# Eight in-place shifts moved behind the last chunk of the lead's second half, and one block's weights fetched later

## The chip, the cores and the metric

The kernel runs on one core of one Trainium2 chip. A core has five engines that run their own instruction lists side by side and wait for one another by semaphores: TensorE (PE, matrix products into the PSUM banks), VectorE (DVE, elementwise work on two operands), ScalarE (ACT, one-operand functions and casts), GpSimd (POOL) and SyncE (SP, which here issues most loads). Loads and stores are DMAs, issued by SP, ACT or POOL. The metric is the device time in microseconds of one execution; a change is read against the median of several.

## The reference

One layer of a streaming encoder, on x of 1024 positions by 1024 channels, in float32. Cut to what matters here:

```python
h = rms_norm(x, norm_mix_g) * (1.0 + sc1) + sh1
proj = h @ w_in                                  # 1024 -> 7168 columns
b_s, c_s, v_s, v_c, gl_c, gate_br = split(proj)
y_a = (b_s * dwconv3(c_s * v_s)) @ w_short_out
y_b = silu(layer_norm(dwconv31(v_c * sigmoid(gl_c)))) @ w_conf_out
g_a, g_b = split(sigmoid(gate_br))
x = x + g1 * ((g_a * y_a + g_b * y_b) @ w_o)
...                                              # SwiGLU ffn, final norm
```

The change sits in the preparation of `h` and the first columns of `h @ w_in`.

## The kernel before, in words

**Layout.** Everything is held transposed: channels on the 128 partitions, positions along the row. The 1024 channels are eight chunks of 128 (KC = 8), the 1024 positions two halves of 512 (`halves`, index h). An operand of a product is kept as a high and a low part (`hi` is a rounding cast on ACT, `lo` the rest, a subtraction on DVE), and `mm3` (lines 386 to 397) makes each product from three matmuls: high by high (L394), low activation by high weight (L395), high activation by low weight (L397). Most of the projection afterwards goes by a scheme of seven products for eight (`PRODUCTS`), which needs sums and differences of chunks k and k + 4 in both halves: `b11`, `b12`, `b21`, `b22`.

**The lead.** Before that scheme can start, the kernel computes some columns directly while x is still being prepared: three column blocks of the gate g_b ("lead", tile names `lead`, gate blocks 0 to 2), and, in the first half, four more. This is the loop `for h in range(2)` at line 845 over `row_blocks` (line 515): per chunk k it asks `act_x` (line 660) for the chunk's activation and `lead_w` or `again_w` (line 709) for its weights, and lists the matmuls of all blocks. In the second half (h = 1) the chunks come in the order `SECOND` = 5, 6, 7, 0, 1, 2, 3, 4: the weights of 5, 6, 7 are still there from the first half (`kept`), those of 0 to 4 are fetched again, 128 x 384 each.

**act_x and modulate.** For a chunk of the second half `modulate` (line 474) lists a DVE multiplication by scale and norm (L476, `x<-x,naff,rx1r`), the high part on ACT (L484, `h41h` for chunk 4, half 1), the low part on DVE (L485, `h41l`), and puts a last step aside in the list `shifts`: the shift of x in place on ACT (L491), which the matmuls of the lead do not need but the sums of the later scheme do. `act_x` decides when the shifts are listed: none after the first four chunks, two after each of the next three, and the remaining two after the last, in the order in which they were put aside.

**Weights.** `next_w(ahead)` (line 355) hands out the next prepared weights after `fetch` (line 360) has brought the list `ready` up to ahead + 1 entries of `plan`. Each entry loads a block from DRAM on SP's queue into a raw buffer (five of them), casts the high part on ACT (L231, `wh<-raw`) and subtracts the low part on DVE (L232, `wl<-raw,wh`); there are three high and three low buffers. The plan in this place is: the five lead blocks of chunks 0 to 4, then one full-width block (`w_plain`, the fourth gate block, 128 x 1024), then the weights of the seven-product scheme. `again_w` asks with ahead = 1 for the first chunks and AHEAD = 2 for the last two.

**What follows the lead.** Line 845 on: after the second half, three activations of the first half that were used unsplit are split (`h00` to `h20`, L426 and L427), the three gate blocks go through a sigmoid on ACT (`sig<-lead`, L578) and out to DRAM. Then the loop at `for k in range(KH)` builds the sums of the scheme (L865, L439, L870) and splits `t2` (L434, L435). Then `col_block(next_w(), hT, (0, 1), "gb")` does the plain gate block: 8 chunks, 2 halves, 3 matmuls, 48 in all, tile name `gb`. Then the scheme starts (tile name `bank`).

**Order of the work.** The kernel is written as one long text; a compiler pass lists each engine's instructions from it. By default what is ready, in the pass's own reckoning, goes in the order of the text; `tc.issue_after(ins)` puts what its block lists on the engine of `ins` behind `ins`, and waits for nothing else. Tiles come from pools with a fixed number of buffers: the large pool `tp` has 58 tiles of 128 x 512, from which h, t2 and their parts are taken. At run time each engine goes through its list in order.

Of the kernel before, what the change touches and what calls it, by code (L numbers as in the profile page):

```python
# [44 lines left out]
KC = D // P  # L45
# [31 lines left out]
KEPT = 3  # L77
SECOND = [*range(KC - KEPT, KC), *range(KC - KEPT)]
# [10 lines left out]
AHEAD = 2  # L89
# [40 lines left out]
def block_kernel(ctx: ExitStack, tc: tile.TileContext, x0, xT, c, vecs, ada, w_first, w_plain, w_duals,  # L130
# [38 lines left out]
    def s_tile(name, dt=F32):  # L169
        return hl_tile(name, dt)  # L170
# [30 lines left out]
    def modc(i):  # L201
        return mod[:, i : i + 1]
# [152 lines left out]
    def next_w(ahead=AHEAD):  # L355

        fetch(ahead + 1)
        return ready.pop(0)

    def fetch(n):  # L360
        while plan and len(ready) < n:
            unit = plan.pop(0)
            ready.append(unit() if callable(unit) else weights(*unit))

    def modulation(i, raw=None):

        if raw is None:
            raw = load(ada[i])
        else:
            nc.sync.dma_start(raw, ada[i])  # L370
        modulation_of(i, raw)
# [8 lines left out]
    def affine(dst, k, sc, gains, g):  # L380
        nc.vector.scalar_tensor_tensor(
            out=dst[:, k : k + 1], in0=modc(sc + k), scalar=1.0, in1=gains[:, g + k : g + k + 1],
            op0=ALU.add, op1=ALU.mult,
        )
# [76 lines left out]
    def rstd_negative(ss, r, q, t=None):  # L461

        t = q if t is None else t
        nc.vector.scalar_tensor_tensor(out=t, in0=ss, scalar=EPS, in1=q, op0=ALU.add, op1=ALU.mult)
        nc.vector.scalar_tensor_tensor(out=r, in0=t, scalar=1.5, in1=r, op0=ALU.subtract, op1=ALU.mult)
        return r
# [7 lines left out]
    def modulate(src, r, scale, shift, name, begun=None, later=None):  # L474

        begin = nc.vector.scalar_tensor_tensor(  # L476
            out=src, in0=src if begun is None else begun, scalar=scale, in1=r, op0=ALU.mult, op1=ALU.mult
        )
        if name is None:
            act = nc.scalar.activation(src, src, AF.Identity, bias=shift)  # L480
            modulate.ins = begin.ins, act.ins, begin.ins
            return None
        hi, lo = hl_tile(name + "h"), hl_tile(name + "l")
        act = nc.scalar.activation(hi, src, AF.Identity, bias=shift)  # L484
        last = nc.vector.scalar_tensor_tensor(  # L485
            out=lo, in0=src, scalar=shift, in1=f32(hi), op0=ALU.add, op1=ALU.subtract
        )
        if later is None:
            nc.scalar.activation(src, src, AF.Identity, bias=shift)
        else:  # L490
            later.append(lambda: nc.scalar.activation(src, src, AF.Identity, bias=shift))  # L491
        modulate.ins = begin.ins, act.ins, last.ins
        return hi, lo
# [48 lines left out]
    def squares_x(src, acc=None, clock=(), tile_of=g_tile):  # L542

        for i, t in enumerate(src):
            sq = tile_of("sq")
            act = nc.scalar.activation(sq, t, AF.Square, scale=1.0 / 32.0)
            if acc is None:
                acc = sq
            else:
                add = nc.vector.tensor_tensor(acc, acc, sq, ALU.add)  # L550
                if i in clock:
                    keep_clock(keep_clock.ins, 1, sq)
                    keep_clock(keep_clock.ins, 1, wide=True)
        squares_x.ins = act.ins, add.ins
        return acc
# [87 lines left out]
    def first_x():  # L643

        nonlocal rx_0
        ss, r, q = rx_0
        y, t = x[0, 0], s_tile("newton")
        begin = nc.vector.scalar_tensor_tensor(out=y, in0=xin[0], scalar=naff1[:, :1], in1=r, op0=ALU.mult, op1=ALU.mult)
        nc.vector.scalar_tensor_tensor(out=t, in0=ss, scalar=EPS, in1=q, op0=ALU.add, op1=ALU.mult)
        keep_clock(keep_clock.ins, 1, t)  # L650
        keep_clock(keep_clock.ins, CLOCK[4], wide=True)
        nc.vector.scalar_tensor_tensor(out=y, in0=t, scalar=1.5, in1=y, op0=ALU.subtract, op1=ALU.mult)
        act = nc.vector.tensor_scalar(y, y, modc(0), None, ALU.add)
        with tc.issue_after(act.ins):
            begin = nc.vector.scalar_tensor_tensor(out=r, in0=t, scalar=1.5, in1=r, op0=ALU.subtract, op1=ALU.mult)
        rx_0 = r
        modulate.ins = begin.ins, act.ins, begin.ins
        return y

    def act_x(k, h=0):  # L660
        nonlocal rx_0, rx_1
        if h == 0:
            with ExitStack() as after:
                after.enter_context(tc.issue_after(squares_x.ins[1] if k in (0, X1_AT + 2) else modulate.ins[0]))
                if k == X1_AT + 2:
                    x1_load.append(act_x.last)
                    after.enter_context(tc.issue_after(x1_load[0]))
                for i in range(2 * k, 2 * k + 2):
                    modulation(i, ucp.tile([P, T + CK - 1], F32, tag="uc", name="ada")[:, :D])
            affine(naff1, k, 8, ng, V_GMIX)  # L670
            x[k, 0] = s_tile(f"x{k}0")
            if k == 0:
                return first_x()
        whole = h == 0 and k < WHOLE
        with tc.issue_after(los[-2]) if len(los) > 1 else ExitStack():
            hT[k][h] = modulate(x[k, h], rx_1 if h else rx_0, naff1[:, k : k + 1], modc(k),
                                None if whole else f"h{k}{h}", None if h else xin[k], shifts if h else None)
        if h:
            los.append(modulate.ins[2])
            for _ in range(len(shifts) if len(los) == KC else 2 * (len(los) > KEPT + 1)):  # L680
                with tc.issue_after(modulate.ins[1]):
                    shifts.pop(0)()
        if h == 0:
            if k == X1_AT:
                for i in range(KC):
                    x[i, 1] = s_tile(f"x{i}1")
                    act_x.last = nc.sync.dma_start(x[i, 1], xT[i, :, halves[1]]).ins
            elif k == X1_AT + 1:
                with tc.issue_after(modulate.ins[2]), tc.issue_after(modulate.ins[1]):
                    rx_1 = squares_x([x[i, 1] for i in range(KC)])  # L690
            elif k == X1_AT + 2:
                with tc.issue_after(modulate.ins[2]):
                    rx_1 = rstd_negative(*rx_1)
            if whole:
                return x[k, 0]
        return hT[k][h]

    los, shifts = [], []
# [10 lines left out]
    def again_w(i):  # L709

        if i < KEPT:
            return kept.pop(0)
        return next_w(1 if i < KC - 2 else AHEAD)

    rx_1 = None
    KH = KC // 2
# [128 lines left out]
    for h in range(2):  # L845
        lead = row_blocks(act_x if h == 0 else lambda i: act_x(SECOND[i], 1), GATES if h else LEAD, "lead", ops,
                          again_w if h else lead_w, 1 + h, None if h else half_way, GATES)
        if h == 0:
            ops = [(again_w(i), xs) for i, xs in ((i, act_x(SECOND[i], 1)) for i in range(3))]
        if h:  # L850
            for k in range(WHOLE):
                with tc.issue_after(modulate.ins[2]):
                    hT[k][0] = split(x[k, 0], hl_tile, f"h{k}0")
        for j, ps in enumerate(lead):
            if j < GATES:
                gate("b", j, h, ps)
            else:
                begun[(j - GATES) // 2]((j - GATES) % 2, "2", ps)
# [746 lines left out]
```

## Time and profile before

| | before |
|---|---|
| median of 3 runs | 1467.25 us (1467.06 to 1467.79) |
| profiled execution | 1467.45 us |
| its span, first to last instruction | 1465.7 us |
| PE busy | 1452.0 us, 99% |
| DVE busy | 1183.8 us, 81% |
| ACT busy | 623.7 us, 43% |
| POOL busy | 503.2 us, 34% |

A line of a timeline reads: start in us from the span's start, duration, engine, line of the kernel, operation, output <- inputs, shapes, count; in brackets the idle time before it and what ended that. Rows with xN are several of a kind merged. Durations of neighbours overlap at their ends, so an instruction's cost in a full engine is the distance to the next start. The views used: the page (busy times), the waits of an engine, and timelines of single engines.

### The profile page before, as it was taken

How to read it: one execution, taken by the hardware profiler on the slowest of the kernel's cores; microseconds unless marked ns; L12 is line 12 of the kernel's file. 1: busy time of each engine (PE TensorE's matmuls, PEld its weight loads, DVE VectorE, ACT ScalarE, POOL GpSimd, SP SyncE). 2: the span in 40 equal slices, each digit the busy share in tenths (PEclk: the TensorE clock that was granted, in tenths of full speed). 3: DMA queues.
4: the chain of work that ended last, by engine and by line, in shares of the span. 5: the costliest groups of instructions: out<-in, count | busy, mean ns of one | idle time of the engine just before them, and what ended most of it. 6: DMA issues, size and time to landing. Idle time of an engine off the chain costs nothing.

```text
span 1465.7 us, 17764 instructions
## 1 busy us (share of the span) xinstructions
PE 1452.0 (99%) x6418; PEld 1192.1 (81%) x6418; DVE 1183.8 (81%) x1643; ACT 623.7 (43%) x911; POOL 503.2 (34%) x459
## 2 busy tenths in 40 slices
PE   9999999999999999999999999999999999999997
PEld 4778888888888888888888888888888888888887
DVE  7897999987988979999688798777777665676755
ACT  4773333333333346455225475444444343222335
POOL 0007777677677761111012002111111015435005
PEclk9999999999999999999999999999999999999999
DMA  9542232323222357486595337655454449989403
GB/s 362 194 138 85 73 101 72 115 72 101 72 87 72 130 201 273 130 256 203 198 322 187 127 116 237 222 184 189 168 173 147 146 154 368 357 279 289 138 8 115
DMA packets 85498, 251.38 MB, mean 172 GB/s; under 512 B 9841, under 2 KB 12529, under 8 KB 85410
## 3 DMA queue, kind: packets, MB, share of 16 engines
q1 hardware_dynamic: 44368, 142.04, 29.2%
q0 software_dynamic: 37008, 95.63, 19.5%
q10 hardware_dynamic: 4034, 12.59, 2.3%
q8 instruction: 50, 0.82, 0.2%
q14 instruction: 38, 0.31, 0.1%
HBM read 187.82 MB, written 62.39 MB: 171 GB/s over the span
## 4 chain that ended last, share of the span: by engine, by line
PE 88%; DVE 1%; POOL 1%; issue 1%; DMA 0%; ACT 0%; POOLq 0%; DVEq 0%
PE bank L397 11%; PE bank L395 11%; PE bank L394 11%; PE x L395 8%; PE x L397 8%; PE x L394 8%; PE z L394 4%; PE z L397 4%; PE z L395 4%; PE y L395 3%; PE y L397 3%; PE y L394 3%; PE mix L397 2%; PE mix L394 2%; PE yb L397 2%; PE yb L394 2%
## 5 line engine op out<-in xcount | busy, mean ns | idle before, releaser
L231 ACT CAST wh<-raw 128x1024 fp32r<-128x1024 f32 (+3 forms) x256 | 256.2, 1003 | 474.3 <-PE bank L395 151.4
L232 DVE TENSOR_TENSOR wl<-raw,wh 128x1024 fp32r<-128x1024 f32 (+3 forms) x177 | 203.0, 1147 | 54.1 <-ACT wh L231 52.7
L232 POOL TENSOR_TENSOR wl<-raw,wh 128x1024 fp32r<-128x1024 f32 x79 | 191.7, 2429 | 105.3 <-ACT wh L231 105.2
L969 DVE SCALAR_TENSOR_TENSOR c<-diff,vec,c 128x512 f32<-128x512 f32 x232 | 168.4, 752 | 2.7
L1319 POOL DMA_DIRECT2D hid<-stage x71 | 37.8, 533 | 344.4 <-DVE stage L435 340.3
L397 PE MATMUL bank<-th,wl 128*128 128x512 f32 x312 | 121.6, 390 | 0.5 <-POOL wl L232 0.5
L394 PE MATMUL bank<-th,wh 128*128 128x512 f32 x312 | 121.5, 389 | 0.0
L395 PE MATMUL bank<-tl,wh 128*128 128x512 f32 x312 | 121.5, 389 | 0.0
L969 DVE SCALAR_TENSOR_TENSOR c<-u,wsum,c 128x512 f32<-128x512 f32 x112 | 84.4, 753 | 2.3
L397 PEld LDWEIGHTS bank<-th,wl 128*128 128x128 f32 x312 | 58.6, 188 | 13.0 <-POOL wl L232 0.9
L394 PEld LDWEIGHTS bank<-th,wh 128*128 128x128 f32 x312 | 58.6, 188 | 12.2
L395 PEld LDWEIGHTS bank<-tl,wh 128*128 128x128 f32 x312 | 58.6, 188 | 12.1
L434 ACT CAST stage<-g 128x512 fp32r<-128x512 f32 x62 | 38.3, 622 | 63.4 <-DMA hid<-stage 42.4
L435 DVE TENSOR_TENSOR stage<-g,stage 128x512 fp32r<-128x512 f32 x62 | 42.6, 690 | 26.7 <-ACT stage L434 26.5
L309 POOL TENSOR_TENSOR raw<-raw 128x1024 f32<-128x1024 f32 x8 | 20.7, 2583 | 110.0 <-ACT th L434 104.8
L1345 POOL DMA_DIRECT2D th<-hid x71 | 38.1, 537 | 53.3 <-PE x L397 34.5
L394 PE MATMUL x<-th,wh 128*128 128x512 f32 x144 | 56.1, 389 | 0.0
L395 PE MATMUL x<-tl,wh 128*128 128x512 f32 x144 | 56.1, 389 | 0.0
L397 PE MATMUL x<-th,wl 128*128 128x512 f32 x144 | 56.1, 389 | 0.0
L395 PE MATMUL yb<-zsl,wh 128*128 128x512 f32 x128 | 49.8, 389 | 0.0
L397 PE MATMUL yb<-zsh,wl 128*128 128x512 f32 x128 | 49.8, 389 | 0.0
L394 PE MATMUL yb<-zsh,wh 128*128 128x512 f32 x128 | 49.8, 389 | 0.0
(818 smaller groups left out, 4173.7 us busy)
## 6 DMA issues: line engine op xcount, KB each, us to landing
hid<-stage POOLq DMA_DIRECT2D x71, 512.0 KB, 4.8
raw<-in_w_duals SPq DMA_DIRECT2D x57, 512.0 KB, 3.5
raw<-in_w_fi SPq DMA_DIRECT2D x54, 512.0 KB, 4.5
th<-hid POOLq DMA_DIRECT2D x71, 256.0 KB, 5.6
tl<-hid POOLq DMA_DIRECT2D x71, 256.0 KB, 5.7
ada<-in_ada SPq DMA_DIRECT2D x24, 512.0 KB, 5.3
raw<-in_ada SPq DMA_DIRECT2D x24, 512.0 KB, 4.5
raw<-in_w_fo SPq DMA_DIRECT2D x24, 384.0 KB, 5.9
```

The lines of the kernel that those rows point to most:

```text
L231: hi = nc.scalar.copy(wh, raw)
L232: lo = lo_engine.tensor_tensor(wl, raw, f32(wh), ALU.subtract)
L309: unit.eng.tensor_tensor(out, x, y, ALU.add)
L394: nc.tensor.matmul(ps, wh, xh, start=first, stop=False, skip_group_check=again)
L395: nc.tensor.matmul(ps, wh, xl, start=False, stop=False, skip_group_check=again)
L397: mm3.ins = nc.tensor.matmul(ps, wl, xh, start=False, stop=last, skip_group_check=again).ins
L434: t_split.act = nc.scalar.copy(hi, src).ins
L435: t_split.ins = nc.vector.tensor_tensor(lo, src, f32(hi), ALU.subtract).ins
L969: tap.ins = nc.vector.scalar_tensor_tensor(out=out, in0=src[:, s : s + H], scalar=wt, in1=acc, op0=ALU.mult, op1=ALU.add).ins
L1319: nc.gpsimd.dma_start(hid_dram[key], s)
L1345: nc.gpsimd.dma_start(t, hid_dram[key][:, s])
```

## The change

It has two parts. In `act_x`, no shift is listed between the chunks of the second half; all eight are listed after the last chunk, behind its high part on ACT, and not in the order in which they were put aside but as chunks 0, 4, 1, 5, 2, 6, 3, 7, in which the sums take them. In `again_w`, the second half's calls ask for one block ahead up to the last but one and for none with the last, so that the plain block's weights, and those of the scheme's first product, are no longer fetched between the chunks but by the later `next_w()` of the plain block, which stands behind the splits, the sigmoids and the loop of the sums.

```diff
-            for _ in range(len(shifts) if len(los) == KC else 2 * (len(los) > KEPT + 1)):
+            if len(los) == KC:
                 with tc.issue_after(modulate.ins[1]):
-                    shifts.pop(0)()
+                    for i in range(KC):
+                        shifts[SECOND.index(i // 2 + i % 2 * KH)]()
@@
         if i < KEPT:
             return kept.pop(0)
-        return next_w(1 if i < KC - 2 else AHEAD)
+        return next_w(1 if i < KC - 1 else 0)
```

## The prediction

> **What bounds the kernel now.** I read the busy times of the page first, then the list of what TensorE (PE) waited for.
>
> ```profile
> PE 1452.0 (99%) x6418; PEld 1192.1 (81%) x6418; DVE 1183.8 (81%) x1643; ACT 623.7 (43%) x911; POOL 503.2 (34%) x459
> ```
> ```profile
> PE bank L397 <- POOL wl L232: 0.5, 1, 0.5
> PE x L395 <- DVE t4l L435: 0.5, 1, 0.5
> PE lead L395 <- DVE h41l L485: 0.3, 1, 0.3
> ```
>
> The first view says that PE is the bound: 1452 us, 99% of the span. The second is the list of PE's waits from 60 us on (total us, times, longest). It has three entries of half a microsecond or less. So there is hardly anything to win behind the start, and whatever holds PE up is paid in full. The third entry is the place that the change aims at. PE's timeline there (start, duration):
>
> ```profile
> 72.22 0.39 PE L394 MATMUL lead<-h31h,wh 128*128 128x512 f32 x1
> ...
> 74.04 0.39 PE L397 MATMUL lead<-h31h,wl 128*128 128x512 f32 x1
> 74.35 0.96 PE L394 MATMUL lead<-h41h,wh 128*128 128x512 f32 x3
> 75.65 0.50 PE L395 MATMUL lead<-h41l,wh 128*128 128x512 f32 x1 [0.34 <-DVE h41l L485]
> ...
> 77.15 0.39 PE L394 MATMUL gb<-h00h,wh 128*128 128x512 f32 x1
> ```
>
> Nine matmuls per chunk start from 72.22 to 74.04, so one starts every (74.04 - 72.22) / 8 = 0.227 us. Ten steps after 74.04 the plain gate block (gb) would start at 76.31; it starts at 77.15. The late low part of the last chunk, h41l, therefore costs **0.84 us**, more than the 0.34 put down as idle. To see why it is late, VectorE (DVE):
>
> ```profile
> 66.46 1.41 DVE L476 SCALAR_TENSOR_TENSOR x<-x,naff,rx1r 128x512 f32<-128x512 f32 x2
> ...
> 73.71 1.23 DVE L232 TENSOR_TENSOR wl<-raw,wh 128x1024 fp32r<-128x1024 f32 x1 [0.39 <-ACT wh L231]
> 74.85 0.75 DVE L485 SCALAR_TENSOR_TENSOR h41l<-x,mod,h41h 128x512 fp32r<-128x512 f32 x1
> ...
> 77.25 0.69 DVE L427 TENSOR_TENSOR h00l<-x,h00h 128x512 fp32r<-128x512 f32 x1
> ...
> 80.79 0.69 DVE L439 SCALAR_TENSOR_TENSOR t<-x,x 128x512 f32<-128x512 f32 x1
> ```
>
> and ScalarE (ACT), whose shifts are the rows of L491:
>
> ```profile
> 65.48 1.34 ACT L491 ACTIVATE x<-x,mod 128x512 f32<-128x512 f32 x2
> ...
> 71.00 1.32 ACT L491 ACTIVATE x<-x,mod 128x512 f32<-128x512 f32 x2
> 72.23 1.45 ACT L231 CAST wh<-raw 128x384 fp32r<-128x384 f32 x2
> 73.58 0.72 ACT L484 ACTIVATE h41h<-x,mod 128x512 fp32r<-128x512 f32 x1
> ...
> 76.38 0.61 ACT L426 CAST h00h<-x 128x512 fp32r<-128x512 f32 x1
> 76.89 0.58 ACT L578 ACTIVATE sig<-lead 128x512 f32<-128x512 f32 x1
> 77.38 0.60 ACT L426 CAST h10h<-x 128x512 fp32r<-128x512 f32 x1
> ...
> 78.93 0.60 ACT L578 ACTIVATE sig<-lead 128x512 f32<-128x512 f32 x1
> 79.43 1.05 ACT L231 CAST wh<-raw 128x1024 fp32r<-128x1024 f32 x1
> ```
>
> The pair of casts at 72.23 is chunk 4's gate weights and the first 1024-wide one, the plain block's; its low part is the DVE row at 73.71, and h41l stands right behind that. Six shifts and the plain block's weights stand ahead of the last chunk. After it, ACT is full until 79.43 + 1.05.
>
> Two things about the order are read from these rows. Of what is ready, each engine has what stands first in the kernel's text: chunk 4's cast and the plain cast, which stand ahead of act_x for chunk 4, are listed ahead of h41h. And tiles of the large pool are given out in the order of the text: at 76.89 a sigmoid runs ahead of h10h although the split stands earlier, because h00l, whose tile comes before h10h's, is only issued at 77.25. The t2 tiles likewise start (80.79) only behind the last of the three splits.
>
> **The change, part by part.**
>
> *Shifts taken from between the chunks.* Six shifts leave the stretch 65.5 to 73.6 of ACT, 0.615 us each by the spacing of the pair at 71.00 (72.23 - 71.00 = 1.23). The last chunk then hangs on DVE: x for chunks 2 and 3 from 66.46 at 0.67 each, h21l, then x for chunk 4, each 0.67, with up to three small weight subtractions of some 0.5 between: x is ready at 69.1 to 70.1. I take 69.7, so h41h ends on ACT at 70.3 and h41l about 71.4. PE needs it at 74.9. The 0.84 us goes: last lead matmul starts at 74.04 + 9 x 0.227 = 76.08 and ends near 76.5.
>
> *Eight shifts behind the last chunk.* ACT from 70.3: chunk 4's cast, 0.40 (the pair at 72.23 takes 1.35 to the next start, of which 0.95 is the wide one), then 8 x 0.615 = 4.92: done at 75.6. Nothing on PE waits for a shift here. The sums that read them (b11 - b12 and so on) stand in the text behind the splits and, by the tile order, could start t2 only behind h20l anyway. Order of need instead of list order: nothing, since DVE's next user comes later than all eight.
>
> *Plain block's weights behind it.* This is the part that costs. The load does not move: it is issued when a raw buffer comes free, and SP has nothing else ahead of it.
>
> ```profile
> 65.44 0.33 SPq L215 DMA_DIRECT2D raw<-in_w_plain  x1
> ...
> 74.96 0.33 SPq L215 DMA_DIRECT2D raw<-in_w_duals  x1
> ```
>
> But the cast and the subtraction now stand in the text behind all eight shifts, the three splits h00 to h20, the three sigmoids of the lead gates, and the t2 loop. In the trace before, three splits and three sigmoids take 79.43 - 76.38 = 3.05 us of ACT in alternation. From 75.6 they end at 78.65, the plain cast (1.03) at 79.7, and PE starts gb 0.05 later, as it started 0.05 behind h41l (74.85 + 0.75 = 75.60, then 75.65). All of gb and all products behind it use weights that are cast later still, so PE has nothing to take in the meantime: it stands from 76.5 to **79.8**. Against 77.15 that is **+2.65 us**: 0.84 won, 3.5 lost.
>
> This order of the plain cast is not in the trace, so bounds. Below: straight behind the shifts, 75.6 + 1.03 + 0.05 = 76.7, or -0.45; if even that were hidden, -0.84. It cannot be much earlier, since it needs one of three high-part buffers, the one that chunk 2's products free at 72.2. Above: the four t2 casts also go first, 0.53 each, +2.1, so +4.8. I take the value with six items ahead, because these stand ahead in the text and are ready by then (the third sigmoid needs the end of the lead at 76.5), while t2 starts only behind h20l.
>
> Behind the plain cast on ACT wait the weights of the next two products; PE needs the first 48 x 0.227 = 10.9 us after gb starts, so they are covered. DVE has to do the plain block's 1.14 us subtraction later too; PE has 32 of gb's 48 matmuls, 7.3 us, that need only the high part. The raw buffer of the plain block comes free some 8 us later, so the load at 74.96 moves to about 83. What comes of it, the low part of the next weights, and its first reader on PE are
>
> ```profile
> 92.69 1.23 DVE L232 TENSOR_TENSOR wl<-raw,wh 128x1024 fp32r<-128x1024 f32 x1
> ```
> ```profile
> 99.93 0.39 PE L397 MATMUL bank<-t2h,wl 128*128 128x512 f32 x1
> ```
>
> so it is ready at 93.9 and used at 99.93: six microseconds of slack, which grows by PE's own delay. I cost the 8 us against the 6.0 + 2.65 at nothing; by this count hardly a microsecond is left over, and each one beyond it would be paid by PE in full (it stands in D).
>
> **Sum.** Profiled execution 1467.45 us (span 1465.7): + 2.65 = 1470.1. The median of the three runs is 0.2 lower, 1467.25, so the forecast is **1469.9 us**, +0.18%. A measurement of this kernel can tell about 0.2%, 2.93 us, from no change, so I forecast no change that counts, on its slow edge.
>
> **Rivals.**
>
> *A, the plain cast slips in early.* If a split waits for its tile or a sigmoid for PE, ACT takes the plain cast two or more items sooner. For it: the row at 76.89 shows such a slip. Against it: DVE is less loaded here than before. gb starts at 76.7 to 79.0, time 1466.8 to 1469.1. Faster by 2.93 us is out of reach: the PE waits from 60 us on and the 0.84 sum to about 2.
>
> *B, slower: the plain cast falls behind t2 casts too*, or the last chunk comes 0.5 us later than I took. Place: ACT between 75 and 81. It decides from gb's start at 80.1 on; with one or two t2 casts ahead 80.3 to 80.9, time 1470.4 to 1471.0.
>
> *C, slower: PE loses speed by standing.* At the start of the trace:
>
> ```profile
> 1.62 4.06 PE L587 MATMUL clock<-ones_r 128*128 128x512 f32 x10 [1.62 <-DVE ones_r L605]
> ...
> 15.20 0.46 PE L587 MATMUL clock<-newton,ones 128*128 128x128 f32 x2 [0.66 <-DVE newton L649]
> 15.42 1.17 PE L587 MATMUL clock<-ones_r 128*128 128x512 f32 x4
> ```
>
> The first ten matmuls start (4.06 - 0.39) / 9 = 0.41 us apart, four of the same kind at 15.42 (1.17 - 0.39) / 3 = 0.26 apart. So there is a slow first stretch that costs 9 x (0.41 - 0.227) = 1.6 us. After a wait of 0.66 us it does not come back; no longer stand than 1.6 us is in the trace, and mine is 3.3. If it comes back: 1469.9 + 1.6 = 1471.5. [...]
>
> *D, something downstream comes late*: the two 0.5 us waits on POOL and DVE in the list above grow, or the weights of the row at 92.69 miss their cover, by half a microsecond to two and a half. 1470.4 to 1472.5.
>
> **How the numbers follow.** Forecast (gb at 79.0 to 80.1, 1469.1 to 1470.2) 0.40; A 0.18; B 0.20; C 0.12; D 0.10. The range leaves out the earliest part of A and the longest of C and D: 1467.5 to 1472.5. Slower by over 0.2% (above 1470.2): B, C and D, 0.42. Within: forecast and most of A, 0.56. Faster: 0.02.
>
> **What would show it.** In the changed profile: h41l off PE's waits, lead's last matmul near 76.1; eight L491 rows in one block from about 70.5 to 76; then PE idle ahead of gb with ACT wh L231 as releaser, 2 to 3.5 us; the 1024-wide cast behind h20h and the sigmoids. Wrong if that cast stands ahead of the splits (A), if t2h stands ahead of it (B), if the matmuls of gb start 0.4 us apart (C), or if PE's waits behind 100 us grow (D).

## The result, and the profile after

The changed kernel takes 1471.45 us (median of 15 runs, 1469.13 to 1474.55); the kernel before, run beside it, 1467.97 us (15 runs, 1466.71 to 1471.02). The ratio is **1.0022, interval 1.0015 to 1.0029**: 3.2 us slower, 2.2 to 4.3. The forecast was 1469.9 in a range of 1467.5 to 1472.5, no change on its slow edge. The direction and the range held. The forecast of +0.18% lies within the interval, and so does 0.2%, so on which side of 0.2% the change lies is not settled.

The profiled execution of the changed kernel has a span of 1469.3 us. First the list of what PE waited for from 60 us on (total us, times, longest):

```profile
PE gb L394 <- ACT h00h L426: 2.5, 1, 2.5
PE bank L397 <- POOL wl L232: 0.6, 1, 0.6
PE x L395 <- DVE t4l L435: 0.5, 1, 0.5
```

The wait for h41l is gone from the list, and a new one of 2.5 us is there, at the place and nearly of the size that the forecast had. But the releaser is not the one that it named. PE waits for **h00h, the first of the three splits**, not for the plain block's weights (`wh L231`). PE's timeline around it:

```profile
77.50 0.39 PE L395 MATMUL lead<-h41l,wh 128*128 128x512 f32 x1
77.72 0.39 PE L397 MATMUL lead<-h41h,wl 128*128 128x512 f32 x1
80.57 0.50 PE L394 MATMUL gb<-h00h,wh 128*128 128x512 f32 x1 [2.46 <-ACT h00h L426]
80.90 0.39 PE L394 MATMUL gb<-h01h,wh 128*128 128x512 f32 x1
...
91.64 0.39 PE L394 MATMUL bank<-h00h,wh 128*128 128x512 f32 x1
```

and ACT's, in which one reads why:

```profile
67.27 0.52 ACT L231 CAST wh<-raw 128x384 fp32r<-128x384 f32 x1 [0.67 <-PE lead L395]
69.31 0.52 ACT L231 CAST wh<-raw 128x384 fp32r<-128x384 f32 x1 [1.52 <-PE lead L395]
69.73 0.72 ACT L484 ACTIVATE h21h<-x,mod 128x512 fp32r<-128x512 f32 x1
71.39 0.51 ACT L231 CAST wh<-raw 128x384 fp32r<-128x384 f32 x1 [0.94 <-ACT h21h L484]
71.81 0.72 ACT L484 ACTIVATE h31h<-x,mod 128x512 fp32r<-128x512 f32 x1
73.43 1.05 ACT L231 CAST wh<-raw 128x1024 fp32r<-128x1024 f32 x1 [0.90 <-ACT h31h L484]
74.39 0.72 ACT L484 ACTIVATE h41h<-x,mod 128x512 fp32r<-128x512 f32 x1
75.01 5.00 ACT L491 ACTIVATE x<-x,mod 128x512 f32<-128x512 f32 x8
79.91 0.60 ACT L426 CAST h00h<-x 128x512 fp32r<-128x512 f32 x1
80.42 1.07 ACT L578 ACTIVATE sig<-lead 128x512 f32<-128x512 f32 x2
```

Three things are to be seen. First, the eight shifts are one block, 75.01 to 79.91, and h00h is behind it. Second, the plain block's cast (the 1024-wide one at 73.43) is not behind the lead at all: it still stands ahead of h41h, although the text fetches it later now. Third, ACT stands idle 0.67, 1.52, 0.94 and 0.90 us where the shifts had been. Each of those waits is a cast listed ahead of the next chunk's high part; of the first two the row names PE, whose matmuls free the buffer that the cast writes. The other two casts begin 0.08 us behind the end of PE's last matmul with the high weights of chunk 1 (h11l, 70.92 + 0.39) and of chunk 2 (h21l, 72.96 + 0.39), so they seem to wait for such a buffer too.

VectorE's list has changed as well. Before, the multiplication that makes chunk 4's x stood ahead of h31l; now it stands behind it. First before, then changed:

```profile
69.96 0.74 DVE L476 SCALAR_TENSOR_TENSOR x<-x,naff,rx1r 128x512 f32<-128x512 f32 x1
...
71.13 0.75 DVE L485 SCALAR_TENSOR_TENSOR h31l<-x,mod,h31h 128x512 fp32r<-128x512 f32 x1 [0.23 <-ACT h31h L484]
```
```profile
72.56 0.75 DVE L485 SCALAR_TENSOR_TENSOR h31l<-x,mod,h31h 128x512 fp32r<-128x512 f32 x1
73.23 0.74 DVE L476 SCALAR_TENSOR_TENSOR x<-x,naff,rx1r 128x512 f32<-128x512 f32 x1
```

So even without the plain cast ahead of it, h41h could not have begun before 73.97; it began at 74.39.

The two executions differ ahead of the change as well (the second half begins at 59.98 before, at 61.17 after; over the ten traces of this case between 58.72 and 61.17, and at 59.86 in the kernel below that only reorders the eight shifts), so I measure from the second half's first matmul (`lead<-h51h`), by start times of PE's timelines, in us. The rows of before that end the stretches are

```profile
76.91 0.40 PE L397 MATMUL lead<-h41h,wl 128*128 128x512 f32 x1
77.15 0.39 PE L394 MATMUL gb<-h00h,wh 128*128 128x512 f32 x1
...
88.14 0.39 PE L394 MATMUL bank<-h00h,wh 128*128 128x512 f32 x1
```

| kernel | second half, to its last lead matmul | from there to gb | gb, to the scheme's first matmul | sum | against before |
|---|---|---|---|---|---|
| before | 16.93 | 0.24 | 10.99 | 28.16 | |
| changed | 16.55 | 2.85 | 11.07 | 30.47 | +2.31 |

So 0.38 is won at the last chunk and 2.61 lost ahead of gb. From the scheme's first matmul to the end of the span it is 1377.5 before and 1377.6 after: nothing comes back later. The trace gives +2.4, the runs +3.2 with an interval that holds both.

### The profile page after: what moved, and what is told of

Same layout as the page of the kernel before. It is cut to its first block, busy times and chain, and to the rows that moved or that the text cites. A ratio compares the mean times of both kernels' runs of the same rounds, so it can differ in the third digit from the quotient of the medians.

```text
span 1469.3 us, 17761 instructions
## 1 busy us (share of the span) xinstructions
PE 1453.4 (99%) x6418; PEld 1192.4 (81%) x6418; DVE 1181.5 (80%) x1643; ACT 625.0 (43%) x911; POOL 503.1 (34%) x459
## 4 chain that ended last, share of the span: by engine, by line
PE 87%; DVE 1%; POOL 1%; issue 1%; DMA 0%; ACT 0%; POOLq 0%; DVEq 0%
PE bank L397 11%; PE bank L394 11%; PE bank L395 11%; PE x L395 8%; PE x L397 8%; PE x L394 7%; PE z L397 4%; PE z L395 4%; PE z L394 4%; PE y L395 3%; PE y L394 3%; PE y L397 3%; PE mix L394 2%; PE mix L395 2%; PE yb L395 2%; PE yb L394 2%
## 5 line engine op out<-in xcount | busy, mean ns | idle before, releaser
L231 ACT CAST wh<-raw 128x1024 fp32r<-128x1024 f32 (+3 forms) x256 | 256.5, 1003 | 472.8 <-PE bank L395 149.1
```

Of the source, the lines that this page charges most:

```text
L231: hi = nc.scalar.copy(wh, raw)
```

## The experiments

Theory S is what the traces suggest: the block of eight shifts stands ahead of h00h. Theory W is the forecast's: the plain weights are cast late. Each ratio is to the kernel before, run beside it, with its 95% interval.

**Part one alone** (the fetch as before).

```diff
-        return next_w(1 if i < KC - 1 else 0)
+        return next_w(1 if i < KC - 2 else AHEAD)
```

> Part one alone: all eight shifts behind the last chunk, weights fetched as before. Theory S (the block of eight shifts stands ahead of the split h00h on ScalarE, and the first matmul of the plain gate block waits for h00h): 2.9 to 3.9 us slower than before (0.20 to 0.27%), PE's wait ahead of gb put down to ACT h00h, 2.5 to 3.5 us. Theory W (the forecast's: what costs is the plain block's weights cast late): the cast is early here as before, so -0.8 to +0.3 us and no wait ahead of gb.

1472.57 us, ratio 1.0043 (1.0029 to 1.0057), 6.3 us slower (4.3 to 8.4). S by its wait, but more than the 2.9 to 3.9 us expected. PE's waits in gb, ACT's timeline, then windows (stretch in us; busy time of PE, PEld, DVE, ACT, POOL with counts; granted clock; DMA share; GB/s), the first of the changed kernel, behind its wait, the others of this one:

```profile
PE gb L394 <- ACT h00h L426: 3.4, 1, 3.4
PE gb L395 <- DVE h00l L427: 0.6, 1, 0.6
```
```profile
73.47 5.00 ACT L491 ACTIVATE x<-x,mod 128x512 f32<-128x512 f32 x8
78.37 1.03 ACT L231 CAST wh<-raw 128x1024 fp32r<-128x1024 f32 x1
79.30 0.61 ACT L426 CAST h00h<-x 128x512 fp32r<-128x512 f32 x1
```
```profile
79.00:83.00 4.00, 2.43 (x10) 1.97 (x11) 3.57 (x6) 4.00 (x9) 0.00 (x0) 1.00 0.31 121
```
```profile
79.00:83.00 4.00, 2.48 (x7) 1.66 (x7) 4.00 (x5) 4.00 (x8) 0.00 (x0) 0.79 0.34 131
83.00:86.00 3.00, 3.00 (x11) 2.27 (x10) 3.00 (x6) 1.32 (x3) 0.00 (x0) 0.71 0.80 262
86.00:90.00 4.00, 4.00 (x20) 3.30 (x19) 4.00 (x8) 1.28 (x3) 0.00 (x0) 1.00 0.00 0
```

The wait grew to 3.4 us because a second wide cast, that of the scheme's first product, now also stands between the shifts and h00h. And behind it the granted clock falls: 0.79 and 0.71, then 1.00 again. That is rival C of the prediction. By the trace this kernel loses 3.25 us against the changed one up to the scheme's first matmul: 0.95 in the wait ahead of gb, and 2.3 in gb, which takes 13.38 us instead of 11.07. Of these 2.3, 0.55 are the wait for h00l in the list, and the rest goes with the slower clock.

**Part two alone** (the shifts as before).

```diff
-        return next_w(1 if i < KC - 2 else AHEAD)
+        return next_w(1 if i < KC - 1 else 0)
```

> Part two alone: weights of the plain block fetched behind the lead, shifts listed between the chunks as before. Theory S: the shifts are the whole cost, so no loss, -0.8 to +0.3 us against before. Theory W: with ScalarE full of shifts between the chunks the plain cast can't slip in ahead and really falls behind the splits, the sigmoids and a t2 cast: gb starts 3 to 4 us later than before, +2.5 to +4 us (0.17 to 0.27%), PE's wait put down to ACT wh L231.

1474.53 us, ratio 1.0048 (1.0035 to 1.0061), 7.0 us slower (5.1 to 8.9): here W happens. PE's waits in gb, then ACT:

```profile
PE gb L394 <- ACT wh L231: 3.5, 1, 3.5
PE gb L397 <- DVE wl L232: 1.1, 1, 1.1
```
```profile
72.21 0.72 ACT L484 ACTIVATE h41h<-x,mod 128x512 fp32r<-128x512 f32 x1
...
73.45 0.60 ACT L426 CAST h00h<-x 128x512 fp32r<-128x512 f32 x1
...
76.08 1.08 ACT L578 ACTIVATE sig<-lead 128x512 f32<-128x512 f32 x2
...
77.96 0.62 ACT L434 CAST t2h<-t 128x512 fp32r<-128x512 f32 x1 [0.80 <-DVE t L439]
78.48 1.99 ACT L231 CAST wh<-raw 128x1024 fp32r<-128x1024 f32 x2
```

With ACT full of shifts between the chunks, the plain cast is behind three splits, three sigmoids and even one t2 cast, as rival B had it. gb starts 3.92 us behind the last lead matmul, 3.7 more than before and within the 3 to 4 expected. What was not expected is gb itself: 14.69 us instead of 10.99, of which 1.07 are the wait for `wl`; the granted clock from 79 to 86 us is 0.50 and 0.53. So neither part is harmless alone, and they are not additive: +6.3 and +7.0 apart, +3.2 together. Part one leaves ACT idle where part two's cast then stands.

**The splits written ahead of the shifts**, all else as in the changed kernel.

```diff
             if len(los) == KC:
+                for j in range(WHOLE):
+                    with tc.issue_after(modulate.ins[2]):
+                        hT[j][0] = split(x[j, 0], hl_tile, f"h{j}0")
                 with tc.issue_after(modulate.ins[1]):
...
-        if h:
-            for k in range(WHOLE):
-                with tc.issue_after(modulate.ins[2]):
-                    hT[k][0] = split(x[k, 0], hl_tile, f"h{k}0")
```

> The changed kernel with the three splits h00 to h20 written ahead of the eight shifts. Theory S: h00h is out some 3 us sooner, PE's wait of 2.5 us ahead of gb is gone, and the time is that of before or up to 0.5 us on either side. Theory W: the splits' place changes nothing for the weights, so as slow as the changed kernel, +3 us against before.

1468.18 us, ratio 1.0005 (0.9997 to 1.0014). The wait ahead of gb is gone, gb follows the lead by 0.23 us (0.24 before). In ACT's list h00h now stands behind two shifts, not eight, and the other two splits stand between the shifts that follow. Of the 3.2 us, 2.5 come back by moving three casts of half a microsecond and their subtractions. What is left is a wait further on, in the scheme's first product, and from that product's first matmul to the end it takes 1378.7 us, 1.2 more than before:

```profile
PE bank L397 <- DVE wl L232: 0.9, 1, 0.9
```

**Four shifts ahead of the splits, four behind** (the loop above entered at i == KH, not ahead of it).

> The changed kernel with four shifts ahead of the three splits and four behind. Theory S by dose: h00h is out 4 x 0.615 = 2.5 us sooner, so the wait of 2.5 us ahead of gb shrinks to 0 to 0.3 us, and the time is that of before, within 0.7 us. If the wait has another cause (the plain weights, the gates), it stays above 1.5 us and the time 2 to 3 us above before.

1468.2 us, ratio 1.0000 (0.9991 to 1.0009). ACT, then PE:

```profile
73.63 2.55 ACT L491 ACTIVATE x<-x,mod 128x512 f32<-128x512 f32 x4
76.08 0.60 ACT L426 CAST h00h<-x 128x512 fp32r<-128x512 f32 x1
```
```profile
76.34 0.39 PE L397 MATMUL lead<-h41h,wl 128*128 128x512 f32 x1
76.74 0.50 PE L394 MATMUL gb<-h00h,wh 128*128 128x512 f32 x1
```

gb starts 0.40 us behind the last lead matmul, against 2.85: four shifts off, 2.45 us less, or 0.61 per shift, as long as one shift takes. The dose fits S. In the first product a `wl` wait of 0.6 appears. The profiled execution is 1.6 us slower than the median of its kernel, and from the scheme's first matmul on it takes 1379.9 us, 2.3 more than before; only 0.8 of that is lost at this wait. So the stretch ahead of gb, not the time of this one execution, is what speaks for S here.

**The order of the eight.**

```diff
-                    for i in range(KC):
-                        shifts[SECOND.index(i // 2 + i % 2 * KH)]()
+                    for shift in shifts:
+                        shift()
```

> The changed kernel with the eight shifts in the order in which they were put aside, not in order of need. Theory S (the first split stands behind all eight shifts, and their number, not their order, is what PE waits for): as slow as the changed kernel, within 0.6 us of it, 3 us slower than before, the wait ahead of gb again 2.5 us. Rival O (the order of need is worth something, the sums start sooner): 0.6 to 2 us slower than the changed kernel.

1471.9 us, ratio 1.0023 (1.0014 to 1.0032), and the wait is the same 2.5 us for h00h. The order of need is worth nothing here that these runs can tell.

**One and three more passes behind the shifts.**

```diff
+                    for i in range(1):  # 3 in the second
+                        nc.scalar.copy(x[i, 1], x[i, 1])
```

> The changed kernel with one more ScalarE pass behind the eight shifts: a copy of one tile onto itself, which changes no value. The wait ahead of gb grows by 0.6 us, to about 3.1 us. Theory S alone: 0.6 us slower than the changed kernel, 3.8 us slower than before. Theory C (a stand of PE that is long enough drops the granted clock to half for some ten matmuls, as after the 3.4 and 3.5 us of the two parts alone): if 3.1 us is enough already, another 1.7 to 2.1 us and a granted clock near 0.5 to 0.8 behind the wait; if not, the clock stays at 1.00.

> The same with three more passes (copies of three tiles onto themselves): the wait ahead of gb grows by 1.8 us, to about 4.3 us. Theory S without a clock effect: 1.8 us slower than the changed kernel, 5 us slower than before. Theory C: the clock falls, so 3.5 to 4 us slower than the changed kernel, 6.5 to 7.5 us (0.45 to 0.51%) slower than before, and the granted clock below 0.8 for some 4 us.

1472.89 us, ratio 1.0030 (1.0018 to 1.0041), and 1473.94 us, ratio 1.0038 (1.0025 to 1.0050). PE's wait and the two windows behind it, with one pass, then with three:

```profile
PE gb L394 <- ACT h00h L426: 3.0, 1, 3.0
```
```profile
79.00:83.00 4.00, 4.00 (x13) 3.10 (x12) 4.00 (x8) 2.63 (x6) 0.00 (x0) 0.60 0.51 197
83.00:86.00 3.00, 3.00 (x14) 2.52 (x13) 3.00 (x7) 2.51 (x4) 0.00 (x0) 0.96 0.00 0
```
```profile
PE gb L394 <- ACT h00h L426: 4.0, 1, 4.0
```
```profile
79.00:83.00 4.00, 3.03 (x7) 2.23 (x8) 3.64 (x7) 3.12 (x7) 0.00 (x0) 0.65 0.30 116
83.00:86.00 3.00, 3.00 (x13) 2.37 (x13) 3.00 (x6) 2.42 (x3) 0.00 (x0) 0.90 0.28 108
```

The clock falls with both. One pass is 4.4 us (2.6 to 6.0) slower than before. With one pass, the stretch from the second half's first matmul to the scheme is 32.53 us, 2.06 longer than in the changed kernel: 0.5 from the pass and 1.54 from gb, which takes 12.61 instead of 11.07 without any further wait. With three it is 34.01. The expected 6.5 to 7.5 us for three passes against before was a little high: +5.85 by the trace, 5.6 (3.7 to 7.3) by the runs.

**The plain block behind the last chunk**, and the scheme's first weights one call later, on the kernel before:

```diff
-    plan += [(w_plain[0], 1024)]
+    plan += [lambda: weights(w_plain[0], 1024, modulate.ins[1:])]
...
-        return next_w(1 if i < KC - 2 else AHEAD)
+        return next_w(1)
```

> The kernel before with one edit: the plain block's cast and subtraction explicitly behind the last chunk's high and low part, and the scheme's first weights fetched one call later. If the plain weights ahead of h41l are what made it late: h41l off PE's waits, 0.5 to 0.84 us faster than before (0.03 to 0.06%). Rival: ScalarE is full there, so PE then waits as long for h00h or the plain cast: 0 to +0.5 us.

1466.02 us, ratio **0.9989 (0.9981 to 0.9998)**, faster than both kernels. PE's whole list of waits from 60 us on, then its timeline where h41l had been late:

```profile
PE bank L397 <- POOL wl L232: 0.5, 1, 0.5
PE x L395 <- DVE t4l L435: 0.5, 1, 0.5
```
```profile
73.28 0.61 PE L394 MATMUL lead<-h41h,wh 128*128 128x512 f32 x2
...
73.96 0.39 PE L395 MATMUL lead<-h41l,wh 128*128 128x512 f32 x1
...
75.32 0.40 PE L397 MATMUL lead<-h41h,wl 128*128 128x512 f32 x1
75.55 0.39 PE L394 MATMUL gb<-h00h,wh 128*128 128x512 f32 x1
```

The second half takes 16.09 us to its last matmul instead of 16.93: the whole 0.84 us that the forecast had worked out. Part two alone, in which the plain weights are also off the last chunk and six shifts still stand ahead of it, takes 16.10. By the runs this kernel is 1.6 us faster than before (0.3 to 2.8). In the trace 0.9 is won up to the scheme's first matmul and 0.3 lost behind it; the interval holds that, and the rest has no place in the trace.

## Why the prediction was right in its time and wrong in its step

*What bounds the kernel, and that a loss ahead of gb is paid in full.* Right for the change: from the scheme's first matmul on it is 1377.5 us before and 1377.6 after, and 1377.4 to 1377.9 in six of the other kernels. Where the splits stand ahead of shifts it is 1378.7 and 1379.9; there PE waits for weights in the first product.

*0.84 us for the late h41l, to be won.* The size was right, as the last experiment shows. Who caused it was half right. I wrote that six shifts and the plain block's weights stand ahead of the last chunk, and let h41h end at 70.3 with the shifts gone. The plain weights alone, moved with the six shifts left in place, give the whole 0.84. With the shifts gone and the plain weights still there, h41h ran from 74.39, or 73.2 on the clock of before (1.19 us subtracted), against 73.58. The sum went by what ACT and DVE had to do and left out that ACT's list, run in order, has a cast ahead of each chunk's high part, and that the cast waits until PE frees a buffer (0.67 and 1.52 us ahead of two of them in the changed kernel). VectorE hangs on the same chain: I let chunk 4's x be ready at 69.7, and it was ready at 73.97, or 72.78 on the clock of before, because its row stood behind h31l. One row of ACT's timeline before says so, and I had not used it:

```profile
68.12 0.52 ACT L231 CAST wh<-raw 128x384 fp32r<-128x384 f32 x1 [0.90 <-PE lead L395]
```

Taking shifts out turned work into waiting. Only 0.38 was won, or 0.39 in part one alone.

*Eight shifts behind the last chunk: "Nothing on PE waits for a shift here."* **This step failed.** No matmul reads a shifted tile soon. (One sum on VectorE does, against what I wrote: at 79.43 it had waited 0.97 us for a shift, but no wait of PE came of it.) But h00h stands behind the block in ACT's list, and PE's next list entry is the matmul with h00h. I had priced the splits as items ahead of the plain cast, and not asked who waits for the first of them. Moving only the splits takes the wait away; halving the block ahead of h00h takes gb's start behind the last lead matmul from 2.85 to 0.40 us.

*Plain block's weights behind it.* **Failed in the changed kernel**, and happened in part two alone. The rule that I read from the rows, that of what is ready the first in the text goes, holds only where several are ready. I take it that in the compiler's reckoning h41h was not ready there, ACT had a hole, and the plain cast took it; the lists show the place, not the reason. Part two alone fits: the shifts fill the holes, and the cast goes where the forecast put it. I had looked for such a slip (rival A) only behind the shifts, never ahead of them, although I had worked out that a buffer for this cast comes free at 72.2: it began at 73.43, or 72.24 on the clock of before.

*The sum.* 3.5 lost less 0.84 won was +2.65; measured by the trace 2.61 less 0.38, and +0.2 of gb and the rest: +2.4. Both terms were too big, by 0.9 and 0.5, and the errors partly cancel. That the first came near is luck. On the clock of before the block of shifts began at 73.8, not at 70.7, 3.1 us late; and from its end to gb it took 0.7 us, with one split, instead of 4.2 with three splits, three sigmoids and the plain cast. The two errors, 3.1 and 3.5, nearly cancel; only the length of the block, 4.9 us, was as forecast.

*Rival C, the clock.* Not in the changed kernel: PE stands 2.46 us, and the windows behind show 1.00. It is there in all four kernels whose PE stands 2.97 us or longer, with a granted clock of 0.50 to 0.79 from 79 to 83 us; between 2.46 and 2.97 nothing was measured. My own forecast of a stand of 3.3 us lies between two, 2.97 and 3.42 us, that met it, and the sum did not price that in. Its size was right: 1.6 in the prediction, 1.54 with one pass. *Rival D* did not happen in the changed kernel: the later waits are 0.6 and 0.5.

## What to carry to other kernels

When a block of work is moved out of the way of one consumer, ask first what stands behind its new place in the same engine's list and who needs that next; that the moved results themselves are not due is no cover (here eight shifts took 4.9 us of ACT, and PE stood 2.46 us for the split behind them). Before pricing freed time on an engine, look for waits that will fill it: here ACT stood idle 0.67 and 1.52 us ahead of two casts whose buffer PE had still to free. And an instruction's place in a compiled list need not be its place in the text, as the plain cast shows, so read the list; two edits that are bad apart (+6.3 and +7.0 us) can be less bad together (+3.2).

## What the runs showed of the hardware

A stand of PE of 3.0 us cost more than 3.0 us here. With 2.46 us of idle time (two kernels) the granted clock behind it stays at 1.00; with 2.97, 3.42, 3.53 and 4.01 us it falls, to 0.60, 0.79, 0.50 and 0.65 from 79 to 83 us, and from 86 to 90 us it is 1.00 again in all four. Behind the 2.97 us matmuls go on 0.23 us apart for about 1.0 us and then 0.43 apart for seven steps, until 83.0; behind the 3.53 they are 0.43 apart or more from the first. A step of 0.43 us is 1.9 times the 0.227 us of before. With 2.97, gb takes 1.5 us longer. The slow stretch lasts 3.0 us there (80.00 to 82.99); after 3.53 us it lasts 5.9 (79.58 to 85.45), with a wait of 1.07 in it. Each of these is the one execution of its kernel that was profiled. No stand between 2.46 and 2.97 us was measured, and what sets the fall and its length no run shows.
